# One hybrid decoder layer on one core: the estimated cost of GpSimd's sums and products in the first phase's scheduler raised from 2.0e-3 to 2.4e-3 per column

## The chip, the cores and the metric

The kernel runs on one core of a Trainium2 chip, as one program. The metric is the device time in microseconds (us), the median of several runs. The instructions are put in order when the kernel is built: a scheduler written in Python decides, with estimated durations, which engine gets which piece of work and in which order each engine's queue holds it. The program holds that order: one list per engine, with waits on semaphores between them.

## The reference

One layer works on 2048 positions of width 1024, in float32. A combined projection feeds two groups of heads side by side:

```python
hn = rms_norm(h, norm1_g)
q, k, v, u = split(hn @ w_in)              # 512 columns each
q, k = partial_rope(q), partial_rope(k)    # the first 16 of 64 dims
# attention: 4 heads x 2 softmax maps of 64 dims, causal, values of 128 dims
attn = (softmax(q1 k1) - lam * softmax(q2 k2)) @ v
attn = rms_norm(attn, subln_g) * (1 - lambda_init)
# state space: 32 groups of 16 channels, a diagonal complex state of 64 per group
x_t = lam_bar * x_{t-1} + B_bar u_t        # associative scan over positions
y = gelu(Re(C x_t) + D u_t)
ssm = y * sigmoid(y @ w_glu + b_glu)
h = h + concat(attn, ssm) @ w_out
hn = rms_norm(h, norm2_g)
h = h + (silu(hn @ w_gate) * (hn @ w_up)) @ w_down   # inner width 2816
return rms_norm(h, final_g)
```

## The kernel before

**Two phases.** The first phase covers the input norm, all projections and the state-space groups; the second covers the gated unit (the sigmoid product above), attention, the output projection and the feed-forward part. Every product of float32 matrices is made as three matmuls of split operands (`mm3`: high by high, high by low, low by high), so each tile that enters a product is first split into a high and a low part by ScalarE and VectorE.

**What sets the order.** `Sched` is a list scheduler. A task has one engine, or several with a cost each; the tasks that it depends on; the rings of buffers that it takes; and a priority (lower goes first). `Sched.run` takes, engine by engine, the task that can start first, with priority deciding between starts that lie within 0.05 us, and adds the estimated cost to that engine's time. So a changed cost moves the estimated times of everything behind it, and with them the order on all engines. Tasks that name both VectorE and GpSimd go where the estimated end, with the cost multiplied by a bias, is earlier: the bias is 4.0 on VectorE in general (`BIAS`) and 1.2 within the state-space pairs (`FAIR`).

In the first phase the code is written as plain calls, and `Rec` records them: `Rec.call` (line 390 on) works out the cost of each call from its operation and its columns n, finds by the memory that it touches what it must follow, and hands it to the scheduler. All these instructions carry line 364 in the profile, since one helper issues them. The second phase gives its tasks costs of its own, which do not go through `Rec.call`.

**What GpSimd does in phase 1.** It makes sums and products of 256 columns while the state-space tables are prepared (`ssm_prep`, twice, for two halves of the groups: tables G, H, W and E, written to DRAM as GD, HD, WD and ED). In each of the 16 state-space pairs it makes six 256-column operations for a table of cosines and sines (`C`, `Sn`, from a small load of ED), and it may take the products `t2`, two of 512 columns per pair, which are open to VectorE and GpSimd.

**A state-space pair** (`ssm_pair(n)`, two groups of channels, priority -50) runs these steps:

- loads of u, G, H, for every other pair of T (from WD), and of ED, all on SP's queue;
- z = G u, six matmuls into bank `pv`, and T u, three matmuls each into `fx` and `tp`;
- four ScalarE copies of z into `pq`; t1 = pq C on VectorE; t2 = pq Sn on VectorE or GpSimd; two sums, two scans, then a second round of t1, t2 and sums on VectorE;
- a split into `xh`, `xl`, twelve matmuls with H onto `fx` and `tp`, a GELU, and a store to yD.

The buffers for u, G, H and ED alternate between pairs, so that pair n can load u when pair n - 2 is through with it; those of pq, t1, t2, xh and xl exist once. In the profile they are all `misc`, banks for projections are `pair`, and the split normalised input is `hn`.

**What lies around the pairs.** The projections of q and k (`proj`, key by key, four tiles of 512 positions, priority -40) are free to go between the pairs' matmuls. A projection tile takes one of four accumulator halves, is split on ScalarE and VectorE, and is stored to qD or kD from one of two store buffers (`up`). One raw weight buffer and three split ones serve the projections' weights, whose loads are urgent (-95). Three keys of q and of k, then half of the values, come before key 0 of q and k, which needs rotary tables. Those reuse the pairs' t1, t2, pq and tr, so that those tiles must follow the last pair's vector work. The second half of the values comes last, with two accumulator halves.

Line 424 holds the one number that is changed: the estimated GpSimd cost of what is neither a product with a scalar nor a memset. `Sched` adds 0.13 us to each GpSimd task and 0.09 to each VectorE task. An operation that reads two tensors in SBUF is marked `port`: its VectorE cost grows where the scheduler has it beside such an operation on GpSimd.

Of the kernel before, what the change touches and what calls it, by code (L numbers as in the profile page):

```python
# [296 lines left out]
class Rec:  # L297
# [88 lines left out]
    @staticmethod  # L386
    def isap(x):
        return hasattr(x, "tensor") and hasattr(x, "ap")

    def call(self, eng, f, args, kw):  # L390
        isap = self.isap
        outs = [kw[n] for n in ("out", "accum_out") if isap(kw.get(n))]
        rest = [x for n, x in kw.items() if n not in ("out", "accum_out") and isap(x)]
        pos = [x for x in args if isap(x)]
        if "out" not in kw:
            outs.append(pos.pop(0))
        ins = rest + pos
        free = lambda x: math.prod(n for _, n in list(x.ap)[1:])
        n = max([free(outs[0])] + ([free(i) for i in ins] if "reduce" in f else []))
        c = ("", f, outs, ins, args, kw)  # L400
        if eng == "pe":
            cost = n / 2400.0 + 0.0035
            if f == "transpose":
                cost = 0.108
            elif kw["rhs"].dtype == F32:
                cost = max(4 * cost, 0.215)
            if self.open and (sum(x[0] for x in self.open) + cost > 1.3
                              or kw.get("start") and self.where(self.open[-1][2][0]) != self.where(outs[0])
                              or self.open[-1][2][0].tensor.name != outs[0].tensor.name):
                self.flush()  # L410
            self.open.append((cost, f, outs, ins, args, kw))
            return None
        self.flush()
        if f == "dma_start":
            return self.task(("sp", 0.47), [c], size=math.prod(outs[0].shape) * 4)
        psum = [x.space == PSUM for x in (outs[0], *ins)]
        if f == "tensor_tensor_scan" or psum[0]:
            dve = 2.3e-3 * n + 0.03
        elif f in ("tensor_scalar", "memset"):
            dve = 0.75e-3 * n + 0.03  # L420
        else:
            dve = 1.06e-3 * n + 0.06 if any(psum) else 1.27e-3 * n + 0.02
        cost = dict(dve=dve, act=0.87e-3 * n + (0.26 if "accum_out" in kw else 0.08),
                    pool=(1.0e-3 if f == "tensor_scalar" else 0.3e-3 if f == "memset" else 2.0e-3) * n + 0.12)
        if kw.get("op") == ALU.pow:
            cost["pool"] += 0.25 + 0.09 * n
        port = f == "tensor_tensor" and not any(psum)
        if eng == "any":
            return self.task({e: cost[e] for e in ("dve", "pool")}, [c], bias=FAIR if self.fair else BIAS, port=port)
        return self.task((eng, cost[eng]), [c], port=port)  # L430
# [1763 lines left out]
```

## Time and profile before

| | before |
|---|---|
| three runs, us | 2423.4, 2428.8, 2435.64 |
| median, us | 2428.8 |
| profiled execution, us | 2427.17 |
| its span, us | 2425.1 |
| granted TensorE clock, mean | 0.984 |
| instructions | 33919 |
| TensorE matmuls, busy us (share) | 2334.0 (96%) |
| VectorE, busy us (share) | 1719.6 (71%) |
| ScalarE, busy us (share) | 1051.0 (43%) |
| GpSimd, busy us (share) | 725.1 (30%) |
| DMA | 435.33 MB, mean 180 GB/s |

The span is what the profiler saw from the first to the last instruction; the execution's own time is 2.1 us longer. By the rows of the trace, the input norm and the projections of u fill the first 90 us; the tables of the state space are prepared until about 233 us; the 16 pairs run to about 406; then come the tiles of q and k with rotary tables and the second half of the values, to about 500. Attention, the gated unit and the output projection follow to about 1160 us, and the feed-forward part to the end. PE is TensorE, DVE VectorE, ACT ScalarE, POOL GpSimd, SP the engine whose queue issues nearly all DMAs. In a row of a trace, `out<-in` are the names of the tiles written and read.

### The profile page before, as it was taken

Reading aid. Unit: us, or ns where it says so; the run is one execution under the profiler, and the core shown is the slowest. Engines: PE = TensorE matmul, PEld = TensorE weight load, DVE = VectorE, ACT = ScalarE, POOL = GpSimd, SP = SyncE. Lnnn points to the kernel's source line nnn. Section 1 sums busy time; section 2 is a strip of 40 time slices with the busy share of each in tenths; the row PEclk is TensorE's granted clock in tenths of the full one; section 3 lists DMA queues with packets and bytes.
Section 4 is the critical chain, followed back from the end, with each engine's and each line's share of the span. In section 5 each row is a group of like instructions: output and inputs, shape, how many; then the busy total and the mean of one; then the engine's idle time right before and its main releaser. Section 6 shows DMA issues by size and latency. Waiting matters only on the chain.

```text
span 2425.1 us, 33919 instructions
## 1 busy us (share of the span) xinstructions
PE 2334.0 (96%) x11832; PEld 1958.8 (81%) x11832; DVE 1719.6 (71%) x2801; ACT 1051.0 (43%) x2103; POOL 725.1 (30%) x824
## 2 busy tenths in 40 slices
PE   7999999889999999998999999999999989999998
PEld 6887798878888888876888888788888868878886
DVE  7885775247887768648987666866666677686787
ACT  7222332247877776545332333533333242242343
POOL 4134675355666556545311000100000010010033
PEclk9999999999999999999999999999999999999999
DMA  6467675665566557786986222522322255574564
GB/s 216 133 189 219 220 223 165 202 215 165 191 197 193 194 188 243 228 293 228 304 270 224 86 83 87 204 92 72 95 85 79 87 179 168 172 258 162 201 213 158
DMA packets 312172, 435.33 MB, mean 180 GB/s; under 512 B 42240, under 2 KB 187712, under 8 KB 312000
## 3 DMA queue, kind: packets, MB, share of 16 engines
q1 hardware_dynamic: 309408, 428.71, 55.5%
q10 hardware_dynamic: 2592, 4.45, 0.5%
q8 instruction: 93, 1.52, 0.3%
q14 instruction: 79, 0.65, 0.1%
HBM read 287.66 MB, written 145.42 MB: 179 GB/s over the span
## 4 chain that ended last, share of the span: by engine, by line
PE 70%; DMA 6%; DVE 5%; issue 3%; ACT 2%; POOL 1%; SPq 0%; POOLq 0%; DVEq 0%; ACTq 0%
PE pair L518 9%; PE pair L519 9%; PE pair L520 9%; PE tp L519 4%; PE tp L520 4%; PE tp L518 4%; PE fx L518 4%; PE fx L519 4%; PE pair L364 4%; PE fx L520 4%; PE pv L518 3%; PE pv L519 3%; PE pv L520 3%; DMA hn<-qD 2%; PE tp L1320 2%
## 5 line engine op out<-in xcount | busy, mean ns | idle before, releaser
L1782 ACT CAST misc<-hn 128x512 fp32r<-128x512 f32 (+1 forms) x340 | 204.9, 609 | 482.8 <-PE pair L519 160.6
L519 PE MATMUL pair<-hn,misc 128*128 128x512 f32 x925 | 361.0, 390 | 6.5 <-DVE hn L1783 4.6
L518 PE MATMUL pair<-hn,misc 128*128 128x512 f32 x925 | 361.3, 391 | 3.2 <-DVE misc L1946 2.5
L520 PE MATMUL pair<-hn,misc 128*128 128x512 f32 x925 | 360.2, 389 | 0.0
L1783 DVE TENSOR_TENSOR misc<-hn,misc 128x512 fp32r<-128x512 f32 (+1 forms) x340 | 237.2, 702 | 82.8 <-ACT misc L1782 82.6
L364 PE MATMUL pair<-hn,misc 128*128 128x512 f32 x1152 | 281.7, 398 | 0.0
L1899 POOL TENSOR_TENSOR misc<-hn 128x512 f32<-128x512 f32 (+1 forms) x13 | 17.9, 1378 | 783.0 <-DVE misc L1783 638.2
L364 PEld LDWEIGHTS pair<-hn,misc 128*128 128x128 f32 x1152 | 214.5, 190 | 45.4 <-issue 2.4
L519 PEld LDWEIGHTS pair<-hn,misc 128*128 128x128 f32 x925 | 173.9, 188 | 44.4 <-DVE hn L1783 6.5
L518 PEld LDWEIGHTS pair<-hn,misc 128*128 128x128 f32 x925 | 174.0, 188 | 41.3 <-DVE misc L1946 3.3
L520 PEld LDWEIGHTS pair<-hn,misc 128*128 128x128 f32 x925 | 173.9, 188 | 36.0
L1221 DVE TENSOR_REDUCE small<-pair 128x1 f32<-128x1024 f32 (+7 forms) x160 | 158.2, 991 | 53.5 <-PE pair L1200 24.8
L1237 ACT ACTIVATE hn<-pair,small 128x1024 f32<-128x1024 f32 (+4 forms) x192 | 166.3, 868 | 59.9 <-DVE small L1228 29.1
L519 PE MATMUL tp<-hn,misc 128*128 128x512 f32 x454 | 178.1, 392 | 3.7 <-DVE hn L1783 3.7
L518 PE MATMUL tp<-hn,misc 128*128 128x512 f32 x454 | 177.8, 392 | 0.0
L520 PE MATMUL tp<-hn,misc 128*128 128x512 f32 x454 | 177.4, 391 | 0.0
L1946 DVE TENSOR_TENSOR misc<-pair,misc 128x512 f32<-128x512 f32 x110 | 75.9, 690 | 84.9 <-PE pair L520 84.6
L364 POOL TENSOR_TENSOR misc<-misc,misc 128x512 f32<-128x512 f32 (+1 forms) x71 | 83.9, 1183 | 166.9 <-DVE misc L364 134.1
L364 DVE TENSOR_TENSOR misc<-misc,misc 128x512 f32<-128x512 f32 (+7 forms) x111 | 92.6, 852 | 36.6 <-ACT misc L364 31.9
L1329 DVE TENSOR_TENSOR hn<-tp,hn 128x512 fp32r<-128x512 f32 x144 | 95.4, 684 | 29.0 <-ACT hn L1326 28.6
L364 POOL TENSOR_TENSOR misc<-misc 128x256 f32<-128x256 f32 (+1 forms) x128 | 100.1, 793 | 43.6 <-DVE misc L364 19.8
L364 PE MATMUL pair<-misc,hn 128*128 128x256 f32 x768 | 103.3, 292 | 8.8 <-DVE misc L364 8.8
(272 smaller groups left out, 5614.7 us busy)
## 6 DMA issues: line engine op xcount, KB each, us to landing
hn<-vD SPq DMA_DIRECT2D x48, 512.0 KB
hn<-kD SPq DMA_DIRECT2D x96, 256.0 KB
hn<-in_w_gate SPq DMA_DIRECT2D x44, 512.0 KB
hn<-in_w_up SPq DMA_DIRECT2D x44, 512.0 KB
fD<-misc SPq DMA_DIRECT2D x88, 256.0 KB
misc<-in_w_down SPq DMA_DIRECT2D x77, 256.0 KB
hn<-qD SPq DMA_DIRECT2D x128, 128.0 KB
hD<-misc SPq DMA_DIRECT2D x32, 512.0 KB
```

Source lines behind the costliest of these rows:

```text
L364: getattr(ENGINE[t.at](self.real), f)(*map(now, args), **{n: now(x) for n, x in kw.items()})
L518: nc.tensor.matmul(out, lhsT=ah, rhs=bh, start=start, stop=False, **k)
L519: nc.tensor.matmul(out, lhsT=ah, rhs=bl, start=False, stop=False, **k)
L520: nc.tensor.matmul(out, lhsT=al, rhs=bh, start=False, stop=stop, **k)
L1221: v.tensor_reduce(out=nl[:, i:i + 1], in_=x.got[sc][:, 0:w], axis=AX.X, op=ALU.max, negate=True)
L1237: a_.activation(out=z.got[rings[i]][:, 0:w], in_=x.got[sc][:, 512 * i:512 * i + w], func=AF.Exp, bias=st(n, n + 1), accum_out=acc)
L1320: nc.tensor.transpose(t4[:, kt, t], a[:, kc % 1024:kc % 1024 + 128], self.ident)
L1329: v.tensor_sub(out=y.got[zr][:, 1], in0=y.got[tp].rearrange("p (k q) -> p k q", k=2), in1=y.got[zr][:, 0].bitcast(F32))
L1782: hf = lambda t: a_.copy(out=dst(t)[0], in_=src())
L1783: lf = lambda t: (g_ if t.at == "pool" else v).tensor_sub(out=dst(t)[1], in0=src(), in1=dst(t)[0].bitcast(F32))
L1899: s1 = any_(n, lambda t, e: e.tensor_tensor(out=t.got[s1r][:, 0:n], in0=q(1, 0), in1=q(1, 1), op=ALU.add), *r, take=[s1r], pri=pri(), bias ...
L1946: return S("dve", 1.042e-3 * w + 0.07, lambda t: v.tensor_tensor(out=(t if to is None else to).got[tm], in0=x.got[bank], in1=y.got[tm], op ...
```

## The change

One coefficient in `Rec.call`:

```diff
         cost = dict(dve=dve, act=0.87e-3 * n + (0.26 if "accum_out" in kw else 0.08),
-                    pool=(1.0e-3 if f == "tensor_scalar" else 0.3e-3 if f == "memset" else 2.0e-3) * n + 0.12)
+                    pool=(1.0e-3 if f == "tensor_scalar" else 0.3e-3 if f == "memset" else 2.4e-3) * n + 0.12)
```

It removes and adds no instruction of TensorE or SP. Some operations that may go to either of VectorE and GpSimd change sides: six products `t2` of 512 columns in the pairs go from GpSimd to VectorE (39 of that form on GpSimd before, 33 now), and in the gated unit four products (lines 1480 and 1496). The order is new on every engine from the preparation of the second half's tables on, and the same again, but for the buffers' names, from TensorE's instruction 4999, VectorE's 1158 (1169 now), GpSimd's 541 (527), ScalarE's 845 (847) and SP's 607 on.

The first place is SP's queue where the state-space stage begins. `misc_1976` (before) and `misc_2021` (now) hold u, G and H; `misc_1805` and `misc_1800` hold ED and its tables; `misc_1983` holds T; kD is the store of a projected k tile from the store buffers `misc_120`; `in_w_v` is a weight load for the values. Before:

```order
L364 DMA HD_73<-misc_122 64x2x256 x2
L364 DMA misc_1805<-ED_76 128x64
L364 DMA WD_75<-misc_122 128x512
L364 DMA misc_1976<-uD_60 128x1x512 x2
L364 DMA misc_1976<-GD_70 128x512
L364 DMA misc_1976<-uD_60 128x1x512 x2
L364 DMA misc_1976<-GD_70 128x512
L364 DMA misc_1976<-HD_72 128x512 x2
L364 DMA misc_1983<-WD_74 128x8x64 x2
```

Now:

```order
L364 DMA kD<-misc_120 8x16x512
L364 DMA misc_1800<-ED_76 128x64
L364 DMA misc_119<-in_w_v 128x1024
L364 DMA kD<-misc_120 8x16x512
L364 DMA WD_75<-misc_122 128x512
L364 DMA misc_2021<-uD_60 128x1x512 x2
L364 DMA misc_2021<-GD_70 128x512
L364 DMA misc_2021<-uD_60 128x1x512 x2
L364 DMA misc_2021<-GD_70 128x512
L364 DMA kD<-misc_120 8x16x512
L364 DMA misc_2021<-HD_72 128x512
```

Two DMAs of k's stores and a weight load of the values have moved in ahead of the first pair's loads of u and G, and two more such DMAs stand among the loads of H, which were in one piece. On TensorE the first matmul with G, the first into `pv`, was instruction 1011 and is 1053: 42 more projection matmuls (into `pair`) stand ahead of it.

The second place is TensorE's queue at the end of the stage. `misc_1983` (now `misc_2024`) holds T, xh and xl, and `misc_1976` (now `misc_2021`) u, G and H. A row names the moving operand first, so `fx<-misc_1983,misc_1976` and `tp_104<-misc_1983,misc_1976`, six matmuls each, are a pair's products with H; the same with the names the other way round, three matmuls each, are products with T; `pv` is z, three matmuls for each of two groups; `pair<-hn` are projections. Products with T of pair n + 1 follow those with H of pair n, since they use the same banks. Before, from pair 15's first z and pair 13's products with H on:

```order
L364 MATMUL pv<-misc_1976 128x256 x3
L364 MATMUL fx<-misc_1983,misc_1976 128x256 x6
L364 MATMUL tp_104<-misc_1983,misc_1976 128x256 x6
L364 MATMUL pair_97<-hn_110,misc_118 128x512 x2
L364 MATMUL pair_97<-hn_111,misc_118 128x512
L364 MATMUL pair_97<-hn_110,misc_118 128x512 x2
L364 MATMUL fx<-misc_1976,misc_1983 128x256 x3
L364 MATMUL pv<-misc_1976 128x256 x3
L364 MATMUL tp_104<-misc_1976,misc_1983 128x256 x3
L364 MATMUL pair_101<-hn_112,misc_118 128x512 x2
L364 MATMUL pair_101<-hn_113,misc_118 128x512
L364 MATMUL pair_101<-hn_112,misc_118 128x512
```

Now, from pair 13's products with T to the first projections behind pair 14's products with H:

```order
L364 MATMUL fx<-misc_2021,misc_2024 128x256 x3
L364 MATMUL tp_104<-misc_2021,misc_2024 128x256 x3
L364 MATMUL pv<-misc_2021 128x256 x3
L364 MATMUL fx<-misc_2024,misc_2021 128x256 x6
L364 MATMUL tp_104<-misc_2024,misc_2021 128x256 x6
L364 MATMUL fx<-misc_2021,misc_2024 128x256 x3
L364 MATMUL tp_104<-misc_2021,misc_2024 128x256 x3
L364 MATMUL pv<-misc_2021 128x256 x3
L364 MATMUL fx<-misc_2024,misc_2021 128x256 x6
L364 MATMUL tp_104<-misc_2024,misc_2021 128x256 x6
L364 MATMUL pair_97<-hn_114,misc_118 128x512
L364 MATMUL pair_97<-hn_115,misc_118 128x512
```

The projections between the pairs are gone: from pair 13's products with T to pair 14's with H nothing else is left, and 20 projection matmuls stand between those and the last pair's products with H, where there were 42 from pair 12's to pair 15's. The last product with H was TensorE's instruction 2018 and is 2038.

## The prediction

> **What bounds the kernel now.** I read the page's head first, then the busy time by stage, then who made TensorE wait, then single rows at the places that the new order touches.
>
> ```profile
> span 2425.1 us, 33919 instructions
> PE 2334.0 (96%) x11832; PEld 1958.8 (81%) x11832; DVE 1719.6 (71%) x2801; ACT 1051.0 (43%) x2103; POOL 725.1 (30%) x824
> ```
>
> TensorE is busy 96% of the span, and the change leaves its matmuls as they are. So only its idle time can move: 2425.1 - 2334.0 = 91.1 us, with what its clock loses behind a pause. The stages (columns: stretch, length, then busy time and count for PE, PEld, DVE, ACT, POOL):
>
> ```profile
> 90.00:232.80 142.80, 139.28 (x664) 115.58 (x662) 107.47 (x280) 35.82 (x77) 52.80 (x73) 0.99 0.64 193
> 232.80:406.50 173.70, 167.76 (x1008) 148.56 (x1008) 125.53 (x177) 61.33 (x142) 108.31 (x110) 0.97 0.70 211
> 406.50:500.00 93.50, 84.62 (x543) 74.98 (x542) 24.91 (x40) 25.76 (x58) 35.37 (x35) 0.96 0.62 193
> 500.00:885.00 385.00, 366.03 (x2374) 318.90 (x2374) 286.44 (x449) 279.43 (x640) 233.42 (x271) 0.98 0.59 188
> ```
>
> The order of instructions differs only from about 90 us to about 885 us: from TensorE's instruction 4999 of 11794 on, all five engines stand in the same order but for buffer names. In that stretch TensorE idles 3.5 + 5.9 + 8.9 + 19.0 = 37.3 us. The second row is the state-space stage (16 pairs, 173.7 / 16 = 10.9 us each). What ended its waits, in 232 to 407 us, then in 406 to 500 and the largest of 500 to 885:
>
> ```profile
> PE pv L364 <- DMA misc<-uD: 5.6, 8, 1.3
> PE pv L364 <- DMA misc<-GD: 3.5, 1, 3.5
> ...
> PE pair L364 <- DVE misc L364: 8.8, 5, 3.0
> ...
> PE pair L1199 <- ACT hn L1237: 9.1, 7, 2.8
> ```
>
> In the state-space stage TensorE waits for loads alone, never for the pairs' own vector work. That is because projection matmuls lie in between and cover it.
>
> **The change, part by part.** The estimate for a GpSimd sum or product of n columns goes from 2.0e-3 n + 0.12 to 2.4e-3 n + 0.12 us, and the scheduler adds 0.13. So 256 columns go from 0.76 to 0.86, and 512 from 1.27 to 1.48. The trace (GpSimd in 230 to 440 us, its 512-column form in the state-space stage alone with least/median/most ns, then VectorE's row for that form):
>
> ```profile
> L364 POOL TENSOR_TENSOR misc<-misc 128x256 f32<-128x256 f32 x83 | 64.7, 792 | 4.1 <-DVE misc L364 1.3
> L364 POOL TENSOR_TENSOR misc<-misc,misc 128x512 f32<-128x512 f32 x39 | 61.2, 1571 | 67.4 <-DVE misc L364 51.1 <-ACT misc L364 12.0 <-PE tp L364 3.7
> L364 POOL TENSOR_TENSOR misc<-misc,misc x27: 1270/1731/1805, 236.0 to 397.8; 128x512 f32<-128x512 f32 x27
> L364 DVE TENSOR_TENSOR misc<-misc,misc 128x512 f32<-128x512 f32 x37 | 33.8, 924 | 15.4 <-ACT misc L364 14.9
> ```
>
> The short form is now over-estimated (0.86 against 0.79), the long one nearer (1.48 against 1.57).
>
> *Six products move.* Six of the state-space stage's 512-column products go from GpSimd to VectorE: 6 x 1.571 = 9.4 us off GpSimd, 6 x 0.924 = 5.5 us onto VectorE, which has 173.7 - 125.5 = 48 us idle there. Taken at nothing. Four products of the gated unit move likewise, with VectorE busy 24.9 of 93.5 us there: nothing. If VectorE's room were gone, 5.5 us would be the price. No DMA is added or removed.
>
> [...]
>
> *The stage starts later.* 42 more projection matmuls stand ahead of the first pair's first matmul. In the rows, the wait is the one with the bracket:
>
> ```profile
> 214.69 14.57 PE L364 MATMUL pair<-hn,misc 128*128 128x512 f32 x63
> 232.77 1.62 PE L364 MATMUL pv<-misc 128*128 128x256 f32 x6 [3.52 <-DMA misc<-GD]
> 234.19 4.04 PE L364 MATMUL pair<-hn,misc 128*128 128x512 f32 x9
> 238.03 0.92 PE L364 MATMUL pv<-misc 128*128 128x256 f32 x6
> 238.79 3.37 PE L364 MATMUL pair<-hn,misc 128*128 128x512 f32 x14
> 241.99 0.75 PE L364 MATMUL fx<-misc,misc 128*128 128x256 f32 x3
> ...
> 225.15 1.30 SPq L364 DMA_DIRECT2D misc<-uD  x2
> 234.27 4.18 SPq L364 DMA_DIRECT2D kD<-misc  x1
> ```
>
> A warm matmul takes (241.99 - 238.79) / 14 = 0.229 us, so TensorE gets there at 229.25 + 42 x 0.229 = 238.9. The loads went out at 225.15 and were ready at 232.77, 7.6 us later. On SP's queue two kD stores and a weight load now stand ahead of them; the fourth tile's store, issued at 234.27 before, is one of those. I put readiness at 236 to 239.4 and leave 0.5 us of the 3.52. The clock is also spared: the nine matmuls after the wait took 238.03 - 234.19 = 3.84 us instead of 2.06, and the six before them 1.62 instead of 0.92, together 2.5. Term: -3.5 - 2.5 + 0.5 = **-5.5** (ends: -6.0, and 0 if SP's queue delays the loads as much as TensorE).
>
> *Early loads of u.* Pair n's u is loaded once pair n - 2's first products are done. Between those and pair 2's first matmul stood 8.5 us of matmuls, now 7.2, and for the next two pairs about 2 us less. The chain that ended last shows what such a load takes:
>
> ```profile
> 321.82 7.52 DMA misc<-uD
> 329.41 8.75 DMA misc<-uD
> ...
> 370.28 6.71 DMA misc<-uD
> ...
> 443.92 8.57 PE pair L364 x48
> 455.17 8.41 DMA vD<-misc
> 464.56 6.03 PE pair L364 x48
> ```
>
> Up to 3 x 1.7 = 5 us more waiting; SP's queue may be freer by then, and the waits before 377 us (4.5) could go. I take **+2** (ends -4.5 and +5), nearer the first three pairs' distances.
>
> *The end of the stage, the term that decides.* The four projection tiles that may run before the stage's buffers are freed (one for each of four accumulator banks) now end before pair 12's carry product. From there to pair 15's the order had 42 projection matmuls and now has 20, all behind pair 14's. Prices per group, from the last pairs before (products with H, then projection, with T, z, T again):
>
> ```profile
> 375.09 0.96 PE L364 MATMUL fx<-misc,misc 64*128 64x256 f32 x6
> 377.12 0.59 PE L364 MATMUL pv<-misc 128*128 128x256 f32 x3 [1.07 <-DMA misc<-uD]
> ...
> 388.31 0.51 PE L364 MATMUL pv<-misc 128*128 128x256 f32 x3
> 388.76 0.62 PE L364 MATMUL fx<-misc,misc 64*128 64x256 f32 x3
> ...
> 390.01 1.43 PE L364 MATMUL pair<-hn,misc 128*128 128x512 f32 x5
> 391.28 0.75 PE L364 MATMUL fx<-misc,misc 128*128 128x256 f32 x3
> 391.93 0.62 PE L364 MATMUL pv<-misc 128*128 128x256 f32 x3
> 392.39 0.86 PE L364 MATMUL tp<-misc,misc 128*128 128x256 f32 x3
> 393.09 4.51 PE L364 MATMUL pair<-hn,misc 128*128 128x512 f32 x19
> ...
> 405.29 0.62 PE L364 MATMUL fx<-misc,misc 64*128 64x256 f32 x3
> ...
> 388.63 1.26 DVE L364 TENSOR_TENSOR_SCAN misc<-r,misc 128x256 f32<-128x256 f32 x2
> 396.42 0.68 DVE L364 TENSOR_TENSOR_SCAN misc<-r,misc 128x256 f32<-128x256 f32 x1
> ```
>
> From start to start: H products 390.01 - 388.76 = 1.25; T products 0.65 + 0.70 = 1.35; three z matmuls 0.46; five projections 1.27. From pair 12's H to pair 15's the new order has 3 x 1.25 + 3 x 1.35 + 4 x 0.46 + 20 projections at 0.25 + one rotation matmul, about 0.5, = 15.1 us of work; before, those pairs took 405.29 - 375.09 = 30.2 us, filled. VectorE's chain cannot go that fast: the last two pairs' scans, undisturbed, are 396.42 - 388.63 = 7.8 us apart, so three steps take 23.4, and TensorE idles 23.4 - 15.1 = 8.3. A second way gives a like number: pair 15's first z follows pair 13's T products at once, where its u load takes 6.71 less the 0.70 of the second T product, 6.0 us. Term: 8.3, less a wait of 1.1 for u that stood there before (at 377.12): **+7.2**. Ends: 6.0 - 1.1 = 4.9, and with the stage's mean pace 3 x 10.9 - 15.1 - 1.1 = 16.5. The undisturbed pace is the nearer row, since the projections that disturb VectorE are gone there.
>
> *The clock behind such a wait.* In the chain above, 48 matmuls took 8.57 us behind the longest wait of that stage, 3.0, and 6.03 at 464.56 us: **+2.5** for one long wait (0 to 5).
>
> *Behind the stage.* 20 fewer projections (4.6 us) are left for the rotary tiles; then the value projections run at the pace of their stores (8.41 us in the chain), so a late start is carried on. The gated unit's products lie more evenly between them now, where TensorE idled 8.8 us. I take **+1** (-4 to +4.6). The attention part to 885 us is dealt anew with the same work; taken at 0 (-4 to +4, against waits of 9.1).
>
> Sum: -5.5 + 2 + 7.2 + 2.5 + 1 = +7.2 us. The profiled execution took 2427.17 us, its span 2425.1 and 2.1 around it, and lies 1.6 below the median of the three runs, 2428.8. So 2434.4 for a profiled execution, and 2428.8 + 7.2 = 2436 as the median. Taken alone this case reaches from 2429 to 2446.
>
> **Rivals.** *Faster:* the end of the stage holds, because pairs 13 to 15 had their vector work done ahead of TensorE, and with truer costs the 5.6 us of waits for u go as well: 2428.8 - 6.0 - 5.6 = 2417. For it: the stage's waits were all loads. Against: 0.7 us of matmuls ahead of a 6.7 us load. It decides if pair 15's first z shows no wait. *Slower by more:* SP's queue eats the gain at the start, early waits cost 5, the end goes at the mean pace (16.5) with two slow-clock spells (5): 2428.8 + 26 = 2455. For it: VectorE also splits two weight tiles there. Against: the 7.8 us of the last scans. *No change:* the value projections, held by stores, take up what the end costs, and the two ends cancel: 2429. For it: 8.8 us of slack there. Against: they start only when the stage has ended. [...]
>
> **Chances.** Forecast 0.48, faster 0.10, slower by more 0.16, no change 0.18, port 0.08. A measurement of this kernel tells about 0.5% (12 us) from no change. Under 2416.7: most of "faster", 0.08. Over 2440.9: "slower by more" 0.16, most of the port 0.06, the forecast's upper end 0.08, so 0.30. Within: 0.62. The range, 2420 to 2453, leaves out about 0.08 below and 0.10 above.
>
> **What the new trace would show.** Right: the first z with under 1 us of wait, near 239 us; pair 15's first z with some 6 us behind a u load; the last H products near 410 us; VectorE with six more 512-column products; every wait after 885 us as before. Wrong: the load of G still waited for, no wait among pairs 13 to 15, or waits of 500 to 885 us that differ by over 5 us.

## The result, and the profile after

The kernel became slower: 2458.55 us (median of four runs, 2455.34 to 2460.61) against 2426.1 (four runs of before, 2423.03 to 2435.64), a ratio of 1.0132 with a 95% interval of 1.0115 to 1.015. That is 32 us, where the prediction had 7.2 and a range that ended at 2453. In the two profiled executions the spans differ by 2458.5 - 2425.1 = 33.4 us. The page of after begins:

```profile
span 2458.5 us, 33905 instructions
PE 2344.7 (95%) x11832; PEld 1963.5 (80%) x11832; DVE 1721.6 (70%) x2812; ACT 1050.6 (43%) x2105; POOL 714.5 (29%) x810
```

TensorE's matmuls are the same 11832, yet they were busy for 10.7 us longer (2344.7 against 2334.0): that part is put down to its clock, 0.980 in the mean against 0.984. Its idle time rose from 91.1 to 113.8 us.

To see where, I took points of TensorE's order that exist in both kernels and compared their times, less the matmuls that the new order has put ahead of the point. Five rows of the timeline of before, and the same five of after: the first matmul with G, the last products with H (three of six on `tp`), the last rotation of a rotary tile, the next wait of a value tile, and the first transposes of the second norm (TensorE's instruction 5617 in both). Before:

```profile
232.77 1.62 PE L364 MATMUL pv<-misc 128*128 128x256 f32 x6 [3.52 <-DMA misc<-GD]
406.09 0.52 PE L364 MATMUL tp<-misc,misc 64*128 64x256 f32 x3
436.65 1.12 PE L364 MATMUL tp<-misc,cst 128*128 128x512 f32 x2
443.92 8.55 PE L364 MATMUL pair<-misc,hn 128*128 128x256 f32 x48 [3.04 <-DVE misc L364]
992.29 0.60 PE L1691 MATMUL tp<-cst,misc 128*128 128x128 f32 x4
```

After:

```profile
242.99 1.65 PE L364 MATMUL pv<-misc 128*128 128x256 f32 x6 [3.46 <-DMA misc<-GD]
424.05 0.52 PE L364 MATMUL tp<-misc,misc 64*128 64x256 f32 x3
453.95 1.02 PE L364 MATMUL tp<-misc,cst 128*128 128x512 f32 x2
463.18 10.68 PE L364 MATMUL pair<-misc,hn 128*128 128x256 f32 x72 [5.10 <-DVE misc L364]
1027.31 0.60 PE L1691 MATMUL tp<-cst,misc 128*128 128x128 f32 x4
```

| point | later by | matmuls ahead of it, more than before | lost up to there | lost since the last point | predicted |
|---|---|---|---|---|---|
| first matmul with G | 10.2 | 42 x 0.229 = 9.6 | 0.6 | 0.6 | -5.5 |
| last product with H | 18.0 | 20 x 0.229 = 4.6 | 13.4 | 12.8 | +2 + 7.2 + 2.5 |
| value tile's wait | 19.3 | none | 19.3 | 5.9 | +1 |
| first transposes of the second norm | 35.0 | none | 35.0 | 15.7 | 0 |
| end | 33.4 | none | 33.4 | -1.6 | 0 |

So the part called decisive came out within about 1 us of its sum, 12.8 for 11.7, though its terms did not come out one by one. The other 25 us that the prediction missed are a gain at the start that did not come (6) and a loss of 21.6 behind the stage, where 1 was taken; 1.6 came back by the end. Of the last 15.7 us, 13.4 had been lost where the two orders agree again: the same matmul starts there at 894.11 us before and at 926.78 after.

**The end of the stage** looks as the prediction drew it. Rows of after from pair 12's products with H to pair 15's:

```profile
393.29 1.28 PE L364 MATMUL fx<-misc,misc 64*128 64x256 f32 x6
394.50 0.62 PE L364 MATMUL pv<-misc 128*128 128x256 f32 x3
395.78 0.63 PE L364 MATMUL pv<-misc 128*128 128x256 f32 x3 [0.66 <-DMA misc<-uD]
...
398.45 1.07 PE L364 MATMUL tp<-misc,misc 128*128 128x256 f32 x3 [0.23 <-ACT misc L364]
403.51 0.98 PE L364 MATMUL pv<-misc 128*128 128x256 f32 x3 [3.99 <-DMA misc<-uD]
...
410.93 0.58 PE L364 MATMUL fx<-misc,misc 64*128 64x256 f32 x1 [1.48 <-ACT misc L364]
412.69 0.79 PE L364 MATMUL fx<-misc,misc 64*128 64x256 f32 x2 [1.18 <-DVE misc L364]
...
414.64 2.50 PE L364 MATMUL pair<-hn,misc 128*128 128x512 f32 x5
...
423.24 0.62 PE L364 MATMUL fx<-misc,misc 64*128 64x256 f32 x3
```

The brackets, from 395.78 on, add up to 7.5 us: waits for u (3.99 for pair 15's), and waits for ScalarE's and VectorE's own work on the pairs, which appear nowhere in this stage before. And the clock fell, from 0.95 in that part before to 0.67. Busy time by stretch, of after (the same part from pair 12's products with H to the end of pair 15's, then the stretches on either side of the clock's fall), and of before from pair 12's products with H to the end of pair 15's (the number behind the busy times is the granted clock):

```profile
393.29:424.57 31.28, 23.64 (x102) 18.71 (x101) 17.46 (x28) 8.45 (x20) 11.42 (x10) 0.67 0.45 124
...
390.00:399.00 9.00, 8.07 (x39) 6.25 (x39) 6.57 (x11) 3.59 (x9) 5.72 (x7) 1.00 0.42 125
399.01:419.49 20.48, 13.78 (x52) 11.29 (x52) 12.95 (x20) 5.95 (x13) 7.80 (x6) 0.50 0.51 131
...
375.09:406.61 31.52, 30.45 (x155) 25.33 (x154) 19.19 (x31) 9.76 (x22) 12.09 (x11) 0.95 0.52 158
```

For 20 us TensorE ran at half its clock (granted 0.50, 399.01 to 419.49 us), with 52 matmuls in it; five projections took 2.50 us (row 414.64), where five took 1.43 before (row 390.01 in the prediction). What made the clock fall at that moment is not shown: by the trace it was 1.00 until 399.0 us and 0.50 from then on, TensorE was busy for 8.07 of the 9.00 us ahead of the fall, and the wait of 3.99 us began only at 403.51 - 3.99 = 399.5.

**The start.** The load of G for the first pair on SP's queue, before, and then the same with what stands ahead of it, after:

```profile
226.50 0.44 SPq L364 DMA_DIRECT2D misc<-GD  x1
```

```profile
228.35 0.60 SPq L364 DMA_DIRECT2D kD<-misc  x1
229.05 0.40 SPq L364 DMA_DIRECT2D misc<-ED  x1
229.54 0.52 SPq L364 DMA_DIRECT2D misc<-in_w_v  x1
230.15 0.62 SPq L364 DMA_DIRECT2D kD<-misc  x1
230.86 0.45 SPq L364 DMA_DIRECT2D WD<-misc  x1
231.41 3.33 SPq L364 DMA_DIRECT2D misc<-uD  x2
234.78 0.68 SPq L364 DMA_DIRECT2D misc<-GD  x1
```

G's load goes out 8.3 us later (234.78 against 226.50), and TensorE gets there 9.6 us of matmuls later. So the wait is 3.46 instead of 3.52, and the six matmuls behind it take 1.65, where they took 1.62 before. The four DMAs ahead of WD's store took 2.5 us of SP's time (228.35 to 230.86), and the loads of u in front of G's took 3.33 us where they had taken 1.30; the last store of HD ahead of them went out at 225.44 where it had been 221.82, 3.6 us later. In GpSimd's new order operations for the first pair's tables stand ahead of the last sums for H; that this is why HD was late is argued, not tested.

**Behind the stage.** The waits of TensorE between the last rotation and the second norm's first transposes, first before (436.65 to 992.29), then after (453.95 to 1027.31); columns: us in total, times, longest:

```profile
PE pair L1199 <- ACT hn L1237: 9.8, 8, 2.8
PE pair L364 <- DVE misc L364: 8.8, 5, 3.0
PE pair L1199 <- DMA hn<-qD: 6.4, 6, 1.8
PE tp L1320 <- DVE hn L1329: 1.5, 2, 0.9
```

```profile
PE pair L1199 <- ACT hn L1237: 14.1, 14, 4.0
PE pair L364 <- DVE misc L364: 9.3, 3, 5.1
PE pair L1199 <- DMA hn<-qD: 8.1, 6, 2.6
PE tp L1320 <- DVE hn L1329: 3.9, 5, 2.2
```

The first row of each is the scores of attention, which wait for the exponentials (line 1237) to free a bank, 14 times instead of 8. By stretch, the same two spans, and a third that an experiment below adds:

```profile
436.65:992.29 555.64, 525.14 (x3467) 461.28 (x3468) 388.94 (x614) 371.08 (x845) 320.36 (x380) 0.98 0.64 201
...
453.95:1027.31 573.36, 531.36 (x3468) 463.28 (x3467) 393.77 (x619) 370.57 (x846) 313.13 (x372) 0.97 0.63 194
...
454.61:1013.78 559.17, 528.60 (x3469) 464.55 (x3468) 388.03 (x616) 369.60 (x843) 317.25 (x377) 0.97 0.64 199
```

With the same matmuls, the second is 17.7 us longer than the first: 11.5 idle, and 6.2 more busy, which is put down to the clock (0.97 against 0.98).

### The profile page after: what moved, and what is told of

The parts are those of the page before. It is cut to its first block, busy times and chain, and to the rows that moved or that the text cites. A ratio compares the mean times of both kernels' runs of the same rounds, so it can differ in the third digit from the quotient of the medians.

```text
span 2458.5 us, 33905 instructions
## 1 busy us (share of the span) xinstructions
PE 2344.7 (95%) x11832; PEld 1963.5 (80%) x11832; DVE 1721.6 (70%) x2812; ACT 1050.6 (43%) x2105; POOL 714.5 (29%) x810
## 4 chain that ended last, share of the span: by engine, by line
PE 65%; DMA 6%; DVE 5%; issue 3%; POOL 2%; ACT 2%; SPq 0%; POOLq 0%; DVEq 0%; ACTq 0%
PE pair L518 9%; PE pair L520 9%; PE pair L519 9%; PE tp L519 4%; PE tp L520 4%; PE tp L518 4%; PE fx L518 3%; PE fx L519 3%; PE fx L520 3%; PE pv L518 3%; PE pv L520 3%; PE pv L519 3%; DMA hn<-qD 2%; PE tp L1320 2%; PE pair L1199 2%
## 5 line engine op out<-in xcount | busy, mean ns | idle before, releaser
L1899 POOL TENSOR_TENSOR misc<-hn 128x512 f32<-128x512 f32 (+1 forms) x13 | 17.5, 1345 | 782.5 <-DVE misc L1783 638.3
L364 POOL TENSOR_TENSOR misc<-misc,misc 128x512 f32<-128x512 f32 (+1 forms) x65 | 76.0, 1170 | 184.7 <-DVE misc L364 142.6
L364 POOL TENSOR_TENSOR misc<-misc 128x256 f32<-128x256 f32 (+1 forms) x128 | 103.9, 824 | 46.4 <-DVE misc L364 19.3
```

The lines of the kernel that those rows point to most:

```text
L364: getattr(ENGINE[t.at](self.real), f)(*map(now, args), **{n: now(x) for n, x in kw.items()})
```

## The experiments

**Theory A** after the result: two losses, each a matter of where matmuls stand. One in the stage, wherever no projection is left between the last pairs; one behind it, since the order of rotary tiles, gated unit and attention is another from there on. **Rival B:** only the late end of the stage costs, and what lies behind is disturbed by the lateness. **Rival C:** the six products on VectorE. **Rival D:** the order of before is a favourable one, and any other costs some 10 us, by no such parts.

Each run is compared with the kernel before, measured beside it on the same chip, and the losses below are against that. First the cost was given to a part of the operations only. Each edit replaces the coefficient on line 424:

```diff
-  2.0e-3
+  (2.4e-3 if n >= 512 else 2.0e-3)                     # 512 columns alone
+  (2.4e-3 if n < 512 else 2.0e-3)                      # 256 columns alone
+  (2.4e-3 if self.pri in (-80.0, -70.0) else 2.0e-3)   # the tables' preparation alone
+  1.9e-3                                               # the cost lowered
```

> The new cost for operations of 512 and more columns alone, the old one for 256. The first matmul with G stands where it stood before (1011); 33, 34, 23, 9 and 20 projection matmuls lie ahead of the products with H of pairs 11 to 15 (before: 47, 28, 31, 24, 18; changed kernel: 24, 18, 0, 0, 20), and from TensorE's instruction 1987 on, behind pair 14's products, the order is the changed kernel's. Theory A (two losses that are both in the order: about 13 us inside the state-space stage, where no projection is left between the last pairs, and about 19 us behind it, in the order of rotary tiles, gated unit and attention): the stage ends as before, within 2 us at equal work, the loss behind it stays, 15 to 20 us, so 2441 to 2446. Rival B (only the late end of the stage costs, and what lies behind merely carries it on): 2426 to 2430.

> The new cost for operations of 256 columns alone. 42 projection matmuls more stand ahead of the first matmul with G, as in the changed kernel; 30, 22, 0, 0 and 20 lie ahead of the products with H of pairs 11 to 15; from 2301 on the order is the changed kernel's. Three products of 512 columns move to VectorE, not six. Theory A: both losses, 2453 to 2460. Rival B: 2453 to 2460 as well. Rival C (the six products that move to VectorE are the cause): about half of it, 2438 to 2446.

> The new cost in the preparation of the state-space tables alone; the pairs are costed as before. The first matmul with G is instruction 1025; 34, 24, 29, 8 and 20 projections lie ahead of the products with H of pairs 11 to 15; no product of the pairs changes engine; behind 2301 the order is the changed kernel's. Theory A: no wait over 2 us among the last pairs, the loss behind the stage stays, 2441 to 2448. Rival B: 2426 to 2432. Rival C: 2426.

> The cost per column lowered from 2.0e-3 to 1.9e-3: another order in the state-space stage (42, 33, 34, 15 and 18 projections ahead of the last products with H), the order of before from TensorE's instruction 2143 on. Theory A: both parts are as before, 2421 to 2432. Rival D (the order of before happens to be a good one, and any other costs 10 us or more): over 2436.

Measured: 2450.31 (ratio 1.0108, 1.0089 to 1.0126), 2461.2 (1.0159, 1.0132 to 1.0185), 2445.69 (1.0086, 1.0068 to 1.0104) and 2424.26 (0.9997, 0.9984 to 1.001). B is out: two kernels with projections ahead of every pair's products with H lost 21 and 26 us all the same. C is no main cause: the preparation's kernel moves no product of the pairs and loses 21 us, while the 512-column one, with seven fewer on GpSimd, loses 11 us less than the 256-column one with three fewer. The 512-column kernel came out 4 us above what A gave, and the 256-column one 1 us. The lowered cost speaks against D as far as the stage goes: its order in the stage is new, and it takes the time of before.

Then a kernel that has the order of after up to a point and that of before behind it, a still higher cost, and two changes to before:

```diff
+  # the gated unit's first product of tile 0 waits for value tile 4's store (after) or tile 8's (before)
-  prev = S("pe", 0.65, products, *ds, *wd, take=...
+  prev = S("pe", 0.65, products, *ds, *wd, *((self.vst[1][4],) if not (b or mm or m or k2) else ()), take=...
+  # line 424 alone
-  2.0e-3
+  2.8e-3
+  # four halves of the store buffers for the value tiles (before)
-  z = turn("up", ups)[:, 0:512].rearrange(...
+  z = turn("up4", ups4).rearrange(...      # ups4: the halves of the two buffers, in turn
```

> The changed kernel with one wait more: the first product of the gated unit may not be put ahead of the store of value tile 4. Up to TensorE's instruction 2241 the order is the changed kernel's, from 2697 on it is that of before (24, not 72, matmuls of the gated unit are dealt in early, 48 before the end of the value tiles). Theory A (what is lost behind the stage is in the order: about 6 us in the rotary tiles, about 13 us in the values and the first attention units): the 13 us are gone, 2442 to 2450. Rival B (attention loses because all of it starts late): 2455 to 2461.

> The cost at 2.8e-3 per column. 22, 0, 0, 0 and 20 projection matmuls lie ahead of the products with H of pairs 11 to 15, so one more pair than in the changed kernel stands bare; 25 of the 512-column operations have left GpSimd, against six in the changed kernel; behind TensorE's instruction 2301 the order is the changed kernel's. Theory A: the stage loses 4 to 5 us more for the bare pair (7.8 us of vector work less 3.1 us of matmuls), 2460 to 2468. Rival E (only the one wait for u counts, not the number of bare pairs): 2455 to 2460. Rival C (products on VectorE cost): over 2470.

> The kernel before, with the gated unit's first product held until the store of value tile 8: the state-space stage is that of before, 24 matmuls of the gated unit stand before the end of the value tiles instead of 48, and all of attention is in a new order. If the loss behind the stage comes from gated-unit matmuls that are used up too early, as theory A has it, holding them back costs nothing or gains: 2414 to 2426. Rival D (any order other than that of before costs): over 2432.

> The kernel before, with the value tiles' store buffers as four halves instead of two: a value tile needs only 512 of a buffer's 1024 columns. The stage ends with 28, 26, 24 and 19 projections between its last pairs, as before. If TensorE's waits among the value tiles (8.8 us before) are for store buffers, they go, with the slow clock behind the longest (2.5): 2412 to 2420. Rival: the value tiles end earlier, and attention, which starts with few units, waits longer instead: 2422 to 2432.

Measured: 2448.6 (1.0097, 1.008 to 1.0114), 2460.78 (1.0147, 1.0132 to 1.0162), 2438.73 (1.0056, 1.0041 to 1.0071), 2445.11 (1.0081, 1.0066 to 1.0096). With the order of before from instruction 2697 on, 10 of the changed kernel's 32 us came back, though it is as late as that kernel: its row is the third of the stretches above, 559.17 us, 3.5 more than before and 14.2 less than after. But the same kind of wait put into before cost 13 us, and the four store buffers cost 19: the value tiles' waits did shrink there (1.8 us left of 8.8 in that group), and more was lost behind them, among others 7.9 us of waits for the second norm's transposes, which are 3.3 us in before. Both misses speak for D as far as the part behind the stage goes. The run at 2.8e-3 came out at the lower end of A's range, and rules C out a second time: 25 products have left GpSimd there, and it is only 2 to 3 us slower than the changed kernel.

To test that A's parts add and that the bare pairs are what counts:

```diff
-  2.0e-3
+  2.5e-3
+  (2.2e-3 if self.fair and n < 512 else 2.0e-3)        # the pairs' 256 columns alone
+  1.7e-3
+  (2.4e-3 if self.pri in (-80.0, -70.0) else 2.0e-3)   # and the gated unit's wait for tile 4
```

> The cost at 2.5e-3 per column. The first matmul with G stands at 1011, as before; 29, 24, 18, 0 and 20 projection matmuls lie ahead of the products with H of pairs 11 to 15 (one bare pair, where the changed kernel has two); from 1987 on the order is the changed kernel's. Theory A: half of the 11.5 us that the changed kernel lost between pairs 12 and 15, and 19 to 20 behind: 2446 to 2454. Rival B: 2430 to 2436. Rival D (any order but that of before costs, by no such parts): no number follows from the order.

> Only the pairs' 256-column operations at 2.2e-3, the rest as before. 36, 32, 28, 19 and 19 projection matmuls lie ahead of the products with H of pairs 11 to 15, so no pair is bare; 15 more projections stand ahead of the last pair's end than before; behind 2301 the order is the changed kernel's. Theory A: the stage loses 0 to 2 us, attention its 13, the rotary tiles 3 to 6: 2440 to 2447. Rival B: 2424 to 2430.

> The cost at 1.7e-3 per column: another order in the state-space stage (34, 23, 36, 24 and 19 projections ahead of the last products with H), that of before from 2019 on. Theory A: nothing lost in either part, 2420 to 2431. Rival D: over 2434.

> The run with the new cost in the preparation of the tables alone (2445.7), with the gated unit's first product held until the store of value tile 4: the stage stays, and from TensorE's instruction 2697 on the order is that of before. Theory A, whose parts add: 2445.7 less the 13 us of attention, 2430 to 2436. Rival (the parts do not add, the gain depends on the stage before): 2440 to 2446.

Measured: 2457.05 (1.0123, 1.0093 to 1.0153), 2453.36 (1.0112, 1.0089 to 1.0136), 2427.18 (0.9998, 0.9985 to 1.0012), 2439.62 (1.0051, 1.0037 to 1.0065). Three of four missed A's totals by 3 to 6 us. The last gave back 6 of the 13 us, or 9 when each of the two kernels is set against the kernel before that was measured beside it. The run at 1.7e-3 hit A's range and missed D's: a new order in the stage cost nothing there.

What holds of A is seen in the parts, not in the totals. A pair with no projection between its products with H and those of the pair ahead is called bare. For each profiled execution, the loss against before up to the last product with H (time, less 0.229 us for each matmul that stands ahead of it more than before), from there to the last rotation (likewise), and from there to the second norm's first transposes:

| kernel | projections ahead of H of pairs 13, 14, 15 | clock, 385 to 425 us | stage | rotary tiles | values and attention | order of attention |
|---|---|---|---|---|---|---|
| before (2.0e-3) | 31, 24, 18 | 1.00 | 0 | 0 | 0 | before's |
| 1.9e-3 | 34, 15, 18 | 1.00 | 1.6 | 1.1 | 4.3 | before's |
| 1.7e-3 | 36, 24, 19 | 1.00 | 1.7 | -0.2 | 1.3 | before's |
| preparation | 29, 8, 20 | 0.96 | -4.2 | 7.2 | 13.2 | after's |
| preparation, gated | 29, 8, 20 | 0.96 | 0.0 | 6.6 | 6.9 | before's |
| pairs, 256 columns at 2.2e-3 | 28, 19, 19 | 1.00 | 3.4 | 6.4 | 19.5 | after's |
| 512 columns | 23, 9, 20 | 0.96 | 5.9 | 3.9 | 16.7 | after's |
| 2.5e-3 | 18, 0, 20 | 0.91 | 10.4 | 3.9 | 16.9 | after's |
| after (2.4e-3) | 0, 0, 20 | 0.74 | 13.4 | 3.9 | 17.7 | after's |
| after, gated at 4 | 0, 0, 20 | 0.79 | 12.4 | 5.6 | 3.5 | before's |
| 256 columns | 0, 0, 20 | 0.79 | 17.5 | 7.3 | 14.5 | after's |
| 2.8e-3 | 0, 0, 20 (and 0 ahead of pair 12's) | 0.62 | 15.0 | 6.4 | 13.1 | after's |

Two executions of the same order up to that point (preparation, and the same gated) differ by 4.2 us in the stage, so a single entry is worth some 4 us. The execution profiled at 1.9e-3 was the slowest of its ten (2433.37 us against a median of 2424.26), so that its row overstates the loss. The stage's loss rises with the bare pairs, in the table from at most 5.9 us with none to 10.4 with one and 12.4 or more with two, and the clock falls with them (0.96 or more, 0.91, 0.79 or less); between two and three the losses overlap. The two ends of the clock's column, the run at 1.7e-3 and the one at 2.8e-3, 385 to 425 us:

```profile
385.00:425.00 40.00, 39.82 (x187) 31.33 (x187) 21.53 (x30) 12.18 (x25) 21.46 (x17) 1.00 0.46 141
```

```profile
385.00:425.00 40.00, 25.26 (x101) 20.44 (x101) 19.79 (x34) 10.13 (x24) 6.00 (x8) 0.62 0.46 124
```

187 matmuls in 40 us against 101. The run at 2.8e-3 also shows that the start's gain exists: its first matmul with G waited 0.78 us, and it lost 3.0 us less than before up to there, so from there to the last product with H it lost 18.0 us against the changed kernel's 12.8, 5.2 more (expected 4 to 5). But the 256-column kernel, with two bare pairs, lost 16.4 in the same part, so the price of a third is not settled. In these twelve rows the losses of values and attention split in two with nothing between: 13.1 to 19.5 us with after's order of attention, whether the stage ended late or not, and 1.3 to 6.9 with before's.

Which property of that order costs? Three more kernels hold other products of the gated unit back in the changed kernel:

```diff
+  # each: one more dependency of the product named, as above
+  (self.vst[1][14],) if b == 1 and mm and not (m or k2) else ()
+  (self.vst[1][7],) if not (b or m or k2) and mm else ()
+  (self.vst[1][3],) if not (b or mm or m or k2) else ()
```

> The changed kernel with the gated unit's fourth product group held until the store of value tile 14. Up to TensorE's instruction 2627 the order is the changed kernel's (72 gated-unit matmuls ahead of the last value tile's end); then fewer are dealt in, 186 by instruction 3000 (changed kernel 215, before 192); from 4436 on the order is that of before. Theory F (what counts is the stock of gated-unit matmuls left when the first long attention units wait for the exponentials): 8 to 14 us are won back, 2444 to 2451. Theory G (the early 72 are what costs): 2455 to 2461. Rival D (any order but that of before costs alike): 2452 to 2465.

> The changed kernel with the second product group of the gated unit held until the store of value tile 7: 48 gated-unit matmuls ahead of the last value tile's end, 193 by instruction 3000, the changed kernel's order up to 2369, that of before from 3822 on. Theory F: 2444 to 2451. Theory G: 2444 to 2451. Rival D: 2452 to 2465.

> The changed kernel with the gated unit's first product held until the store of value tile 3: 42 gated-unit matmuls ahead of the last value tile's end, 185 by instruction 3000, the order of before from 4436 on. Theory F: 2444 to 2451. Theory G: 2444 to 2451. Rival D: 2452 to 2465.

Measured: 2455.4 (1.0132, 1.0113 to 1.0151), 2452.88 (1.012, 1.01 to 1.0141) and 2469.77 (1.0181, 1.0153 to 1.0209). Theory F (what counts is the stock of gated-unit matmuls that is left) missed all three. Theory G (the early ones are what costs) hit the first, missed the second by 2 us and fell with the last, which has fewer early matmuls of the gated unit than before (42 against 48) and about the stock of before by instruction 3000 (185 against 192), and is the slowest of all. D's range held twice and ended 5 us too low for the last. The stretch of that slowest kernel behind the last rotation, and its waits:

```profile
457.88:1038.38 580.50, 536.26 (x3469) 467.48 (x3468) 388.58 (x616) 368.18 (x840) 317.28 (x379) 0.96 0.62 191
```

```profile
PE pair L1199 <- DMA hn<-qD: 10.4, 6, 2.6
PE pair L1199 <- ACT hn L1237: 9.4, 10, 4.1
```

It waits less for the exponentials than after (9.4 against 14.1) and more for the loads of q (10.4 against 8.1). Of the 7.1 us by which this stretch is longer than in after, only 2.2 are idle; in the other 4.9 TensorE is busy, at a granted clock of 0.96 instead of 0.97. So with one and the same stage ahead of it, attention in five orders (gated at 4, 7, 14, after's own, gated at 3) took 3.5, 10.5, 12.8, 17.7 and 24.9 us more than in before, one execution each. For this part rival D fits: the order of before is the cheapest of those seen. That the order is the cause is shown by the two kernels that got the order of before back there (3.5 us left of 17.7, and 6.9 of 13.2); which property of the other orders costs stays open, since no single count of mine tells them apart. No kernel tried beat before; the two with a lowered cost equal it.

## Why the prediction was wrong

- **The step that failed most** is "The attention part to 885 us is dealt anew with the same work; taken at 0 (-4 to +4, against waits of 9.1)." It measured 15.7 us between the value tile's wait and the second norm (13.4 of them where the order is new), and 13 to 20 behind the last rotation in every kernel with that order. The bound of 4 was set against waits of 9.1 us, as if a new order could only shuffle the waits that are there. The gated runs put the scatter of that part at over 20 us. Its own sign was named ("waits of 500 to 885 us that differ by over 5 us"), and that sign came: TensorE's waits there went from 18.4 us to 28.6 in the same part of after (518 to 917 us).
- **The start**, -5.5, was mis-sized: +0.6. The end "0 if SP's queue delays the loads as much as TensorE" is what happened: 8.3 us on SP against 9.6 on TensorE. Readiness "at 236 to 239.4" was 242.99. I had counted SP's extra DMAs but not that the store of HD ahead of them would go out 3.6 us later, nor that the loads of u would hold SP for 2.0 us longer; why they did is not shown.
- **The end of the stage and its clock**, 7.2 + 2.5, came out in place and kind, and near in sum. From pair 12's products with H to the last of pair 15's the new order took 424.57 - 393.29 = 31.3 us, the old one 406.61 - 375.09 = 31.5, with 53 projection matmuls more in it (51 x 0.229 + 2 x 0.12 = 11.9 us): a loss of 11.5 to 11.7 for the 9.7. The prediction and the section on the change say 42 projections from pair 12's products to pair 15's; 42 is the count from pair 13's, from pair 12's there were 73. The sum did not use it, since it set the new order's work against the vector work's pace. The two terms were less near than their sum: TensorE's idle time there grew by 7.6 - 1.1 = 6.6 us for the 7.2, and the clock took some 5 for the 2.5 (23.64 us busy, against 30.45 - 11.9 = 18.5 for the same work before). The wait for pair 15's u was 3.99, not 6.0, and the clock stood at 0.50 for 20 us. That the stage came within 1 us is in part luck, since entries of one order differ by some 4 us.
- **Early loads of u**, +2: 12.8 less 11.5 leaves 1.3, but not by that path. TensorE's waits for u between the first matmul with G and pair 12's products with H fell, from 4.5 us to 3.0; new there are 1.3 for ScalarE and 1.7 with no cause that the profile shows.
- **Behind the stage**, +1, measured 5.9: two rotations waited for ScalarE's copies (3.6 us in all, none before), and the value tile's wait grew from 3.04 to 5.10. The prediction's paragraph said that 20 fewer projections are left there; that they were the missing cover is argued, not tested, and the bound of 4.6 was too narrow.
- **Six products to VectorE**, nothing: not contradicted. The kernel without any of them lost as much behind the stage; up to 6 us in the stage for the 512-column run, which moves seven, are not told apart from its thin fill (9 ahead of pair 14's).
- Of the rivals, "slower by more" had the right size (2455) by luck, for the place was mostly wrong: that SP's queue eats the gain at the start came, and some 5 us by the clock, but the rest was put into the stage's end at its mean pace and into early waits, neither of which came. "Faster" fell with the wait of 3.99 us at pair 15's first z. The sign "the last H products near 410 us" did not follow from the prediction's own terms, which give 406.1 + 4.6 + 6.2 = 416.9; it was 424.05. What the chances call port, a loss on GpSimd from the six products, is not seen as a cost: in the stage GpSimd's 256-column form went from 792 ns (230 to 440 us of before) to 838 (239 to 450 us of after, the first two rows below), which is 83 x 0.046 = 3.8 us on an engine that idles there, and in the preparation's kernel, where no product moved, it took 831 (third row, 230 to 440 us).

```profile
L364 POOL TENSOR_TENSOR misc<-misc 128x256 f32<-128x256 f32 x83 | 68.4, 838 | 9.0 <-DVE misc L364 3.4 <-DMA misc<-ED 2.6
L364 POOL TENSOR_TENSOR misc<-misc,misc 128x512 f32<-128x512 f32 x29 | 47.3, 1631 | 82.8 <-DVE misc L364 57.7 <-ACT misc L364 22.6 <-PE tp L364 2.1
...
L364 POOL TENSOR_TENSOR misc<-misc 128x256 f32<-128x256 f32 x83 | 68.0, 831 | 7.8 <-DVE misc L364 4.9
```

## What to carry to other kernels

A number in a scheduler's cost table acts through the order that it produces, not through its truth: a value nearer the trace for the 512-column form (not for the 256-column one) was 32 us slower here, while 1.7e-3 and 1.9e-3 gave the time of 2.0e-3. Where a new order deals out a stage with many waits, such as attention here, its cost has to be bounded by how much such orders differ (over 20 us here), not by the waits of the old one; and a point where the order becomes the same again says about where the loss lies (13.4 of the 15.7 us here), not how large it is. Cover is a stock: projections that an estimate spends on the early pairs are missing at the last ones, and TensorE then lost here both the waits (7.5 us from pair 12 on) and, for 20 us, half its clock (0.50).

## What was not expected of the hardware

The granted clock followed the fill closely in the twelve profiled executions of the table: over the same 40 us it was 0.96 to 1.00 with no bare pair, 0.91 with one, 0.74 to 0.79 with two and 0.62 with three. What a single wait cost in clock was less regular. At the first matmul with G a wait of 3.46 us in after was followed by six matmuls at 1.65 us, and a wait of 4.05 us at the same place in the gated run (at 4) by the same six at 0.97. The clock fell to 0.50 in both: from 241.99 us on for 6.83 us in after, and in the gated run from 243.79 on for 3.41, 0.8 us after its wait had ended, so that the projections behind the six were slowed instead (ten took 4.04 us, where fourteen took 3.37 in before at 238.79). The kernel at 1.7e-3 waited 3.41 us there and kept its clock at 1.00. In the gated run, then after, the gated run again, and the run at 1.7e-3:

```profile
242.96 0.97 PE L364 MATMUL pv<-misc 128*128 128x256 f32 x6 [4.05 <-DMA misc<-GD]
...
241.99:248.82 6.83, 5.83 (x17) 4.86 (x18) 1.40 (x3) 2.06 (x5) 1.79 (x1) 0.50 0.76 244
...
243.79:247.20 3.41, 3.41 (x11) 2.65 (x10) 0.69 (x1) 1.47 (x4) 1.63 (x1) 0.50 0.78 270
...
233.14 0.95 PE L364 MATMUL pv<-misc 128*128 128x256 f32 x6 [3.41 <-DMA misc<-GD]
229.73:236.00 6.27, 2.86 (x16) 2.52 (x16) 1.38 (x3) 1.78 (x5) 1.90 (x2) 1.00 0.91 240
```

So in these three executions the wait's length alone did not say what the clock would cost: 6.83 us at 0.50 with a wait of 3.46, 3.41 us at 0.50 with one of 4.05, none with one of 3.41.
